# One encoder layer on one core: the delta rule's chunk step written as an affine map, and the head sums of keys and queries moved into the projection banks

## The chip, the cores and the metric

The kernel runs on one core of one Trainium2 chip. The metric is the device time of one execution in microseconds (us), the median of several runs. TensorE (PE) multiplies matrices into PSUM, which has eight banks of 128 x 512 numbers of 32 bits; VectorE (DVE) and ScalarE (ACT) work element by element and read PSUM; GpSimd (POOL) does the same between SBUF tiles, and the DMA queues move data between HBM and SBUF. PE's weight loads are listed apart, as PEld.

## The reference, cut to what matters

One layer of a streaming encoder for 1024 prompt frames and 64 sample frames. After a norm, one combined projection feeds four mixers in parallel (a conv module, a gated delta rule, a multi-scale pool, stick-breaking attention). Their outputs are concatenated, projected and added; a SwiGLU feed-forward follows. The change touches the scan of the delta rule and the norm of the attention's keys and queries.

```python
def chunk_gated_delta(q, k, v, g, beta, S0):
    ...
    sol = lax.linalg.triangular_solve(lmat + jnp.eye(CHUNK, dtype=jnp.float32), rhs,
                                      left_side=True, lower=True, unit_diagonal=True)
    u_c, w_c = sol[..., :Dv], sol[..., Dv:]
    ...
    def step(S, xs):
        u_i, w_i, attn_i, q_i, k_i, gl = xs
        v_new = u_i - jnp.einsum('bhcd,bhde->bhce', w_i, S)
        o = jnp.einsum('bhcd,bhde->bhce', q_i, S) + jnp.einsum('bhij,bhje->bhie', attn_i, v_new)
        S = S * gl[..., None, None] + jnp.einsum('bhcd,bhce->bhde', k_i, v_new)
        return S, o

def stick_breaking_mixer(u, k_prev, v_prev, qn_g, kn_g):
    B, L, _ = u.shape
    qkv = u.reshape(B, L, 3, SB_HEADS, SB_HEAD_DIM).transpose(2, 0, 3, 1, 4)
    q = rms_norm(qkv[0], qn_g)
    k = rms_norm(qkv[1], kn_g)
    ...
```

A chunk has 64 frames, there are four heads of width 64.

## The kernel before, in words

The frames are worked in two halves: half A is the first 512 prompt frames, half B the other 512 and the 64 of the sample. The program is written as: input projection of A, norm of B, mixers of A, input projection of B, mixers of B, output projection and feed-forward of A, then of B. A scheduler with a model of the machine decides the order in which the instructions of each engine stand, so projections of one half stand between the mixer steps of the other. Each engine executes its instructions in that order.

A projection (`gemm_fm`, tile `pg`) makes 128 output features in one PSUM tile for each piece of columns: one of 512 for half A, two of 288 for half B. Each operand is split into a high and a low part, so 8 blocks of input features give 24 matmuls. `gemm_bank` hands out the banks: at first the two of the pool `ps_mm`. The attention has three banks (`ps_sb`), the delta rule two (`ps_dn`, used through `PD` and `PS`), and `ps_cv` is a single bank, handed out by `PC`:

```python
    def PC(name):
        return ps_cv.tile([P, 512], F32, tag="cv", name=name)
...
            pm = PC("pmu")
...
            pm = PC("pvar")
...
                pp = PC("ppl")
```

These three tiles are the conv's mean and variance and the pool's small projection. A tile of a pool is handed out in the order of the program text, and the next use of the bank waits until the last has been read.

For keys and queries (`sb_qk`, four tiles to a half) ScalarE copies the projection to `qk` and its square to `qksq`; a matmul with a block of ones (`pqk`) sums the squares of a head, and ScalarE takes logarithm and exponent of it for the norm.

The delta rule (`delta`, `dn_group`) works groups of four chunks, two groups to a half, and one group of one chunk for the sample. A group makes the products of keys and queries (`pkk`, `pkq`), transposes keys and values by matmuls with an identity (`pkt`, `pvt`, and later `pw` from `X`, `pof`), and solves a triangular system: its diagonal blocks go by DMA to a layout that GpSimd solves row by row, and come back as `X`; the levels above are done by batches of matmuls (`pw`, `py`, `px`). `batch` issues 16 matmuls of 64 x 64 for four chunks, one for each chunk and head. Then `u` (`pu`) and the transposed `w` (`pwt`) are made, and the recurrence goes chunk by chunk: `pvn` = w S, `vn` = u - `pvn`, `pkv` = k `vn`, and the state S is scaled by ScalarE and added to by VectorE; the output `po` gathers q S and attention times `vn`.

Of the kernel before, what the change touches and what calls it, by code (L numbers as in the profile page):

```python
# [7 lines left out]
F32 = mybir.dt.float32  # L8
# [51 lines left out]
def hybrid_encoder_kernel(ctx: ExitStack, tc: tile.TileContext, io):  # L60
# [41 lines left out]
    def PC(name):  # L102
        return ps_cv.tile([P, 512], F32, tag="cv", name=name)
# [9 lines left out]
    def act_(out, in_, func, bias=0.0, scale=1.0):  # L113
        nc.scalar.activation(out, in_, func, bias=bias, scale=scale)  # L114

    def copy_a(out, in_):
        nc.scalar.activation(out, in_, ACTF.Copy)  # L117
# [4 lines left out]
    def tt(out, a, b, op):  # L122
        nc.vector.tensor_tensor(out=out, in0=a, in1=b, op=op)  # L123
# [13 lines left out]
    def mm(out, lhsT, rhs, start=True, stop=True):  # L137
        return nc.tensor.matmul(out, lhsT=lhsT, rhs=rhs, start=start, stop=stop)  # L138

    def mms(out, lhsT, rhs, start=True, stop=True):  # L140
        nc.tensor.matmul(out, lhsT=lhsT, rhs=rhs, start=start, stop=stop, skip_group_check=True)  # L141
# [193 lines left out]
    def gemm_bank(name="pg"):  # L335
        turn[0] += 1
        pool, tag = BANKS[turn[0] % 8] if wide[0] else BANKS[0]
        return pool.tile([P, 512], F32, tag=tag, name=name)
# [54 lines left out]
    def sb_qk(h):  # L393
        n_ = h.n
        for pi, piece in enumerate(("k", "q")):
            for m in range(2):
                ada_step(ADA_B if h.samp else ADA_N)
                t, sq = ST("qk"), ST("qksq")
                lo = ST("qkl") if piece == "k" else t
                tiles = gemm_fm(h, io["wfm"][14 + 2 * pi + m], h.hi, h.lo, KALL)  # L400
                with tc.high_priority():
                    for ps, c0, n in tiles:
                        copy_a(t[:, c0:c0 + n], ps[:, 0:n])
                        act_(sq[:, c0:c0 + n], ps[:, 0:n], ACTF.Square)
                    for c0, n in h.chunks:
                        pn = PC("pqk")
                        mm(pn[:, 0:n], C("bdones"), sq[:, c0:c0 + n])
                        act_(sq[:, c0:c0 + n], pn[:, 0:n], ACTF.Ln, bias=epst, scale=1.0 / 64)
                    act_(sq[:, 0:n_], sq[:, 0:n_], ACTF.Exp, scale=-0.5)
                    stt(t[:, 0:n_], t[:, 0:n_], gqk[:, pi:pi + 1], sq[:, 0:n_], ALU.mult, ALU.mult)  # L410
                    copy_a(sq[:, 0:n_].bitcast(F32R), t[:, 0:n_])
                    d = sbd[piece, h.name]
                    if piece == "k":
                        nc.sync.dma_start(out=io["sbk"][m, :, h.row0:h.row0 + n_], in_=t[:, 0:n_])
                    tt(lo[:, 0:n_].bitcast(F32R), t[:, 0:n_], sq[:, 0:n_], ALU.subtract)
                    for x, v in enumerate((sq, lo)):
                        if piece == "k":
                            for y in range(2):
                                nc.sync.dma_start(out=d[2 * m + y, 64 * x:64 * x + 64], in_=v[64 * y:64 * y + 64, 0:n_])
                        else:  # L420
                            nc.sync.dma_start(out=d[128 * m:128 * m + 128, x], in_=v[:, 0:n_])
# [265 lines left out]
    def dn_group(h, feats, gate, D, ch0, nch, tok0, mtok0, S):  # L687
# [7 lines left out]
        def v4(t):  # L695
            return t[:, 0:w].rearrange("p (a c d) -> p a c d", a=2, c=nch)
# [10 lines left out]
        def PS(name):  # L707
            return PD(name)
# [108 lines left out]
        batch(pwt, blk(kbe), blk(Y))  # L817
        wT = T4("X")
        copy_a(wT[:, 0:w], pwt[:, 0:w])
        po = ps_dn.tile([P, 512], F32, tag="dn", name="po")  # L820
        u4, o4 = v4(u), v4(po)
        for c in range(nch):
            pv2 = PS("pvn")
            for pair in range(2):
                j = (pair * nch + c) * 64
                for hp in range(2):
                    r = slice(64 * hp, 64 * hp + 64)
                    mm(pv2[r, pair * 64:pair * 64 + 64], wT[r, j:j + 64], S[r, pair])
                    mms(po[r, j:j + 64], qd[r, j:j + 64], S[r, pair], c == 0 and pair == 0, False)
            vn = dn.tile([P, 2, 64], F32, tag="vn", name="vn", bufs=2)  # L830
            tt(vn, u4[:, :, c], pv2[:, 0:128].rearrange("p (a d) -> p a d", a=2), ALU.subtract)
            for pair in range(2):
                act_(S[:, pair], S[:, pair], ACTF.Copy, scale=D["gl"][:, pair, ch0 + c:ch0 + c + 1])
            pk2 = PS("pkv")
            for pair in range(2):
                j = (pair * nch + c) * 64
                for hp in range(2):
                    r = slice(64 * hp, 64 * hp + 64)
                    mm(pk2[r, pair * 64:pair * 64 + 64], kup[r, j:j + 64], vn[r, pair])
                    mms(po[r, j:j + 64], at[r, j:j + 64], vn[r, pair], False, True)  # L840
            tt(S, S, pk2[:, 0:128].rearrange("p (a d) -> p a d", a=2), ALU.add)
        sq = T4("Y")
        act_(sq[:, 0:w], po[:, 0:w], ACTF.Square)
        ss = sm.tile([P, 2, 4], F32, tag="oss", name="oss")
# [510 lines left out]
```

## Time and profile before

| what | value |
|---|---|
| median of 3 runs | 1529.09 us (1527.38 to 1532.03) |
| the profiled execution | 1532.56 us, of it 1530.8 us from the first to the last instruction (span) |
| PE busy | 1459.6 us, 95% of the span |
| weight loads busy | 1259.9 us, 82% |
| VectorE busy | 1030.5 us, 67% |
| ScalarE busy | 663.2 us, 43% |
| GpSimd busy | 88.3 us, 6% |
| mean granted clock of TensorE | 0.953 of full speed |

Full speed is 2.4 GHz; the granted clock is a mean over a stretch, in which the engine runs at full or at half speed. A busy time is a sum over the whole span, in which stages with different limits follow one another; a busy PE also counts time at half clock, and the ends of pipelined matmuls. What a stage is worth is therefore read from windows, with the clock beside the busy time.

### The profile page before, as it was taken

How to read it: one execution, taken by the hardware profiler on the slowest of the kernel's cores; microseconds unless marked ns; L12 is line 12 of the kernel's file. 1: busy time of each engine (PE TensorE's matmuls, PEld its weight loads, DVE VectorE, ACT ScalarE, POOL GpSimd, SP SyncE). 2: the span in 40 equal slices, each digit the busy share in tenths (PEclk: the TensorE clock that was granted, in tenths of full speed). 3: DMA queues.
4: the chain of work that ended last, by engine and by line, in shares of the span. 5: the costliest groups of instructions: out<-in, count | busy, mean ns of one | idle time of the engine just before them, and what ended most of it. 6: DMA issues, size and time to landing. Idle time of an engine off the chain costs nothing.

```text
span 1530.8 us, 24538 instructions
## 1 busy us (share of the span) xinstructions
PE 1459.6 (95%) x9688; PEld 1259.9 (82%) x9688; DVE 1030.5 (67%) x1816; ACT 663.2 (43%) x1191; POOL 88.3 (6%) x196
## 2 busy tenths in 40 slices
PE   7899999958998989999999999999999999999999
PEld 5777799835896857677878778789899999999998
DVE  7877999865379997666766588744655555555554
ACT  4446554645454567466676442222432222222221
POOL 0000400030003000200300000000000000000000
PEclk7999999968897999699999999999999999999999
DMA  8796677432354213252323477622322222222222
GB/s 287 262 295 208 207 223 236 121 75 90 117 178 145 70 45 93 82 153 84 107 91 91 131 268 260 210 95 86 135 70 84 83 83 84 83 83 84 83 84 103
DMA packets 106867, 205.41 MB, mean 134 GB/s; under 512 B 39360, under 2 KB 49024, under 8 KB 106752
## 3 DMA queue, kind: packets, MB, share of 16 engines
q1 hardware_dynamic: 99936, 193.36, 39.1%
q0 software_dynamic: 6816, 10.49, 3.1%
q8 instruction: 76, 1.25, 0.3%
q14 instruction: 39, 0.32, 0.1%
HBM read 175.57 MB, written 28.24 MB: 133 GB/s over the span
## 4 chain that ended last, share of the span: by engine, by line
PE 70%; issue 11%; DMA 7%; DVE 6%; POOL 3%; ACT 2%; SPq 1%; DVEq 0%; POOLq 0%; ACTq 0%
PE pg L138 59%; PE psC L141 2%; POOL fst L135 1%; POOL fsu L135 1%; PE pw L138 1%; DVE junk L212 1%; PE psO L141 1%; PE z L141 1%; DVE wlo L123 1%; DMA out_sbk_dram<-qk 1%; DMA wadt<-in_wadat_dram 1%; DMA X<-xd 1%; DMA fsn<-nld 1%; DVE xA L126 1%; DVE nrm L126 1%
## 5 line engine op out<-in xcount | busy, mean ns | idle before, releaser
L138 PE MATMUL pg<-hi,whi 128*128 128x288 f32 (+1 forms) x1504 | 504.8, 336 | 7.6 <-ACT vf L117 3.3
L138 PE MATMUL pg<-hi,wlo 128*128 128x288 f32 (+1 forms) x1504 | 500.6, 334 | 4.8 <-DVE wlo L123 4.8
L138 PE MATMUL pg<-lo,whi 128*128 128x288 f32 (+1 forms) x1504 | 502.5, 334 | 1.7 <-DVE lo L126 1.6
L117 ACT ACTIVATE whi<-wraw 128x1024 fp32r<-128x1024 f32 (+2 forms) x192 | 199.7, 1041 | 488.2 <-PE pg L138 422.4
L138 PEld LDWEIGHTS pg<-hi,whi 128*128 128x128 f32 x1504 | 287.1, 191 | 35.5 <-ACT vf L117 4.1
L138 PEld LDWEIGHTS pg<-hi,wlo 128*128 128x128 f32 x1504 | 286.4, 191 | 29.9 <-DVE wlo L123 6.8
L138 PEld LDWEIGHTS pg<-lo,whi 128*128 128x128 f32 x1504 | 287.2, 191 | 27.9 <-issue 3.3
L123 DVE TENSOR_TENSOR wlo<-wraw,whi 128x1024 fp32r<-128x1024 f32 (+2 forms) x192 | 230.9, 1203 | 106.6 <-ACT whi L117 105.4
L138 PE MATMUL pg<-g,whi 128*128 128x288 f32 (+1 forms) x1056 | 253.1, 332 | 0.1
L138 PEld LDWEIGHTS pg<-g,whi 128*128 128x128 f32 x1056 | 180.0, 190 | 14.8 <-ACT acc L114 0.6
L138 PE MATMUL pg<-g,wlo 128*128 128x288 f32 (+1 forms) x528 | 173.1, 331 | 0.0
L126 DVE SCALAR_TENSOR_TENSOR xs<-pg,mod,xs 128x288 f32<-128x288 f32 (+2 forms) x288 | 106.5, 413 | 85.7 <-PE pg L138 82.5
L138 PEld LDWEIGHTS pg<-g,wlo 128*128 128x128 f32 x528 | 100.1, 190 | 7.8
L123 DVE TENSOR_TENSOR fa<-fa,pg 128x288 f32<-128x288 f32 (+1 forms) x66 | 35.0, 531 | 101.4 <-PE pg L138 98.2
L126 DVE SCALAR_TENSOR_TENSOR cy<-cvb,vec,cy 128x512 f32<-128x512 f32 (+1 forms) x120 | 94.2, 799 | 0.2
L126 DVE SCALAR_TENSOR_TENSOR xA<-pg,mod,xA 128x512 f32<-128x512 f32 x96 | 70.6, 747 | 22.8 <-PE pg L138 22.6
L212 DVE CUSTOM_DVE_ANT_0 junk<-wads,cb,vec 128x1024 bf16<-128x1024 f32 x32 | 41.0, 1282 | 17.6 <-DMA wads<-in_wadat_dram 12.8
L114 ACT ACTIVATE e<-e 128x512 f32<-128x512 f32 (+4 forms) x100 | 51.9, 519 | 0.8
L212 DVE CUSTOM_DVE_ANT_0 junk<-wadt,cb,vec 128x1024 bf16<-128x1024 f32 x32 | 41.0, 1282 | 16.3 <-DMA wadt<-in_wadat_dram 16.2
L138 PE MATMUL pg<-mixs,whi 128*128 128x288 f32 x256 | 50.9, 295 | 0.0
L114 ACT ACTIVATE zs<-zs 128x512 f32<-128x512 f32 (+4 forms) x50 | 25.7, 514 | 36.8 <-DVE zs L123 35.7
L138 PEld LDWEIGHTS pg<-mixs,whi 128*128 128x128 f32 x256 | 41.0, 188 | 0.1
(304 smaller groups left out, 1922.7 us busy)
## 6 DMA issues: line engine op xcount, KB each, us to landing
wraw<-in_wgate_dram SPq DMA_DIRECT2D x44, 512.0 KB, 3.7
wraw<-in_wup_dram SPq DMA_DIRECT2D x44, 512.0 KB, 3.8
wraw<-in_wdown_dram SPq DMA_DIRECT2D x44, 512.0 KB, 3.6
wadt<-in_wadat_dram SPq DMA_DIRECT2D x32, 512.0 KB, 5.0
wads<-in_wadat_dram SPq DMA_DIRECT2D x32, 512.0 KB, 4.5
wraw<-in_wfm_dram SPq DMA_DIRECT2D x30, 512.0 KB, 4.3
wraw<-in_wout_dram SPq DMA_DIRECT2D x16, 512.0 KB, 3.7
xA<-in_xa_dram SPq DMA_DIRECT2D x16, 256.0 KB, 6.7
```

The lines of the kernel that those rows point to most:

```text
L114: nc.scalar.activation(out, in_, func, bias=bias, scale=scale)
L117: nc.scalar.activation(out, in_, ACTF.Copy)
L123: nc.vector.tensor_tensor(out=out, in0=a, in1=b, op=op)
L126: nc.vector.scalar_tensor_tensor(out, a, s, b, op0, op1)
L135: nc.gpsimd.tensor_tensor(out=out, in0=a, in1=b, op=op)
L138: return nc.tensor.matmul(out, lhsT=lhsT, rhs=rhs, start=start, stop=stop)
L141: nc.tensor.matmul(out, lhsT=lhsT, rhs=rhs, start=start, stop=stop, skip_group_check=True)
L212: nc.vector.tensor_tensor_reduce(out=junk, in0=w, in1=cbt[g], scale=1.0, scalar=V("b_ada", col), op0=ALU.mult, op1=ALU.add, accum_out=mod[ ...
```

## The change

It has two parts. In `sb_qk` the head sum's tile comes from `gemm_bank` instead of `PC`. In `dn_group` the step over a chunk becomes an affine map of the state: S' = k u + M S with M = gl I - k w, and M is made for all four chunks at once (`pww` is w itself, `pmt` is k w, `gi` the scaled identity, `mt_` the difference). The loop over chunks holds the two matmuls of the map, summed in PSUM (`pst`), and one copy to the next state; all states stay in `Sc`. What hung on the states (`pvn`, `vn`, `po`) then follows in batches.

```diff
@@ sb_qk
-                        pn = PC("pqk")
+                        pn = gemm_bank("pqk")
                         mm(pn[:, 0:n], C("bdones"), sq[:, c0:c0 + n])
@@ dn_group
-        po = ps_dn.tile([P, 512], F32, tag="dn", name="po")
-        u4, o4 = v4(u), v4(po)
+        pw2 = PS("pww")
+        batch(pw2, blk(Y), blk(kbe))
+        wt_ = T4("W")
+        copy_a(wt_[:, 0:w], pw2[:, 0:w])
+        gi = T4("vb")
+        tt(v4(gi), bc(D["gl"]), C("sel2")[:, 0:64].unsqueeze(1).unsqueeze(1).to_broadcast(sh4), ALU.mult)
+        pm = PS("pmt")
+        batch(pm, blk(wt_), blk(kup))
+        mt_ = T4("Y")
+        tt(mt_[:, 0:w], gi[:, 0:w], pm[:, 0:w], ALU.subtract)
+        Sc = T4("kbe")[:, 0:128 * nch].rearrange("p (c a d) -> p c a d", c=nch, a=2)
+        copy_a(Sc[:, 0], S)
+
+        def each(c):
+            for pair in range(2):
+                for hp in range(2):
+                    yield pair, slice(64 * hp, 64 * hp + 64), (pair * nch + c) * 64
+
         for c in range(nch):
-            pv2 = PS("pvn")
-            for pair in range(2):
-                j = (pair * nch + c) * 64
-                for hp in range(2):
-                    r = slice(64 * hp, 64 * hp + 64)
-                    mm(pv2[r, pair * 64:pair * 64 + 64], wT[r, j:j + 64], S[r, pair])
-                    mms(po[r, j:j + 64], qd[r, j:j + 64], S[r, pair], c == 0 and pair == 0, False)
-            vn = dn.tile([P, 2, 64], F32, tag="vn", name="vn", bufs=2)
-            tt(vn, u4[:, :, c], pv2[:, 0:128].rearrange("p (a d) -> p a d", a=2), ALU.subtract)
-            for pair in range(2):
-                act_(S[:, pair], S[:, pair], ACTF.Copy, scale=D["gl"][:, pair, ch0 + c:ch0 + c + 1])
-            pk2 = PS("pkv")
-            for pair in range(2):
-                j = (pair * nch + c) * 64
-                for hp in range(2):
-                    r = slice(64 * hp, 64 * hp + 64)
-                    mm(pk2[r, pair * 64:pair * 64 + 64], kup[r, j:j + 64], vn[r, pair])
-                    mms(po[r, j:j + 64], at[r, j:j + 64], vn[r, pair], False, True)
-            tt(S, S, pk2[:, 0:128].rearrange("p (a d) -> p a d", a=2), ALU.add)
+            pS = PS("pst")
+            for pair, r, j in each(c):
+                mms(pS[r, pair * 64:pair * 64 + 64], kup[r, j:j + 64], u[r, j:j + 64], pair == 0, False)
+            for pair, r, j in each(c):
+                mms(pS[r, pair * 64:pair * 64 + 64], mt_[r, j:j + 64], Sc[r, c, pair], False, True)
+            nxt = S if c == nch - 1 else Sc[:, c + 1]
+            copy_a(nxt, pS[:, 0:128].rearrange("p (a d) -> p a d", a=2))
+        pv2 = PS("pvn")
+        for c in range(nch):
+            for pair, r, j in each(c):
+                mm(pv2[r, j:j + 64], wT[r, j:j + 64], Sc[r, c, pair])
+        vn = T4("W")
+        tt(vn[:, 0:w], u[:, 0:w], pv2[:, 0:w], ALU.subtract)
+        po = PS("po")
+        o4 = v4(po)
+        for c in range(nch):
+            for pair, r, j in each(c):
+                mms(po[r, j:j + 64], qd[r, j:j + 64], Sc[r, c, pair], c == 0 and pair == 0, False)
+        for c in range(nch):
+            for pair, r, j in each(c):
+                mms(po[r, j:j + 64], at[r, j:j + 64], vn[r, j:j + 64], False, True)
```

Since the scheduler sets the order, it moves far more than these lines. First, PE's order in half A's second delta group, from the attention's steps to the first use of the solved `X` (the `pw` with a number; `z`, `psC` and `psO` are the attention, `pvar` the conv). Before:

```order
L138 MATMUL pvar<-cvs,cst 128x256 x2
L141 MATMUL psC<-sl,u_r 128x384
L141 MATMUL z<-q_2693,k_2691 128x128 x2
L141 MATMUL z<-neg_r,id_r 128x128
L141 MATMUL psC<-sh,omu_r 128x384
L141 MATMUL psC<-sl,omu_r 128x384
L141 MATMUL psO<-zs,v_2594 64x384
L141 MATMUL psC<-sh,u_r 128x512
L141 MATMUL psC<-sl,u_r 128x512
L728 MATMUL pw_2130<-cst,X 64x64
```

The same place of the change:

```order
L138 MATMUL pvar<-cvs,cst 128x256
L138 MATMUL pg<-hi_1356,whi 128x288
L138 MATMUL pg<-lo_1357,whi 128x288
L138 MATMUL pg<-hi_1356,wlo 128x288
L138 MATMUL pg<-hi_1364,whi 128x288
L138 MATMUL pg<-lo_1365,whi 128x288
L138 MATMUL pg<-hi_1364,wlo 128x288
L138 MATMUL pg<-hi_1372,whi 128x288
L138 MATMUL pg<-lo_1373,whi 128x288
L138 MATMUL pg<-hi_1372,wlo 128x288
L138 MATMUL pg<-hi_1380,whi 128x288
L141 MATMUL z<-q_2775,k_2773 128x128
```

Between the last `pkk` of this group and that `pw` stand 2 projection matmuls (`pg`) before and 167 of the change. In the second group of half B there are 45 before and 114 of the change, in its first group 48 of 512 columns and 72 of 288 before and 126 of 512 of the change.

Second, PE's order in half A at its first key tile, whose last matmul is `pg<-hi_564,wlo`. The row with + is the head sum, which stood behind the next tile's 24 matmuls:

```order
 L138 MATMUL pg<-lo_565,whi 128x512
 L138 MATMUL pg<-hi_564,wlo 128x512
+L138 MATMUL pqk<-qksq,cst 128x512
 L138 MATMUL pg<-hi_277,whi 128x512
 L138 MATMUL pg<-lo_278,whi 128x512
```

Third, PE's order in the recurrence of half A's first group. Before, one chunk's first half (`X` is the tile that holds w by then):

```order
L138 MATMUL pg<-hi_1340,wlo 128x288
L138 MATMUL pvn<-S_p,X 64x64
L141 MATMUL po<-S_p,qd 64x64
L138 MATMUL pvn<-S_p,X 64x64
L141 MATMUL po<-S_p,qd 64x64
L138 MATMUL pvn<-S_p,X 64x64
L141 MATMUL po<-S_p,qd 64x64
L138 MATMUL pvn<-S_p,X 64x64
L141 MATMUL po<-S_p,qd 64x64
L141 MATMUL psC<-sh,u_r 128x384
```

Of the change, the end of one chunk's map and the beginning of the next (`nl` is the tile that holds u, `kbe` the one of the states):

```order
L138 MATMUL pg<-lo_1373,whi 128x288
L141 MATMUL pst<-kbe,Y 64x64 x4
L141 MATMUL pst<-nl,kup 64x64 x4
L141 MATMUL psC<-sh,omu_r 128x384
L141 MATMUL psC<-sl,omu_r 128x384
L138 MATMUL pg<-hi_1372,wlo 128x288
```

A chunk had two such blocks of eight; it now has one, with 30 or so projection and attention matmuls to the next. Blocks of 64 x 64 matmuls between wider ones number 83 in PE's whole order before and 95 of the change. GpSimd's order changes in one place: the solve of half A's second group stood behind the loads of all four heads of the attention, and now stands ahead of the fourth head's.

## Rows read from the trace of the kernel before

**Rows 1.** Windows: length, busy us (instructions) by engine, clock, DMA share, GB/s.

```profile
100.00:304.40 204.40, 201.73 (x1543) 169.23 (x1541) 177.12 (x324) 115.41 (x235) 21.70 (x39) 0.98 0.66 208
304.40:400.00 95.60, 68.22 (x585) 47.57 (x583) 53.13 (x120) 44.24 (x97) 15.44 (x37) 0.76 0.31 86
...
458.90:660.00 201.10, 188.73 (x1220) 141.99 (x1220) 170.30 (x290) 114.53 (x219) 26.01 (x66) 0.86 0.30 88
...
1120.00:1530.80 410.80, 406.91 (x3068) 406.67 (x3068) 205.08 (x393) 93.53 (x127) 0.00 (x0) 1.00 0.26 86
```

**Rows 2.** Timeline of PE: start, duration, operation, count, idle before and releaser.

```profile
304.40 0.29 PE L138 MATMUL pg<-hi,wlo 128*128 128x288 f32 x1
...
341.39 0.31 PE L728 MATMUL pw<-cst,X 64*64 64x64 f32 x1 [10.32 <-DMA X<-xd]
343.79 0.47 PE L138 MATMUL pw<-cst,X 64*64 64x64 f32 x2 [2.08 <-DMA X<-xd]
...
372.34 0.65 PE L138 MATMUL pqk<-qksq,cst 128*128 128x288 f32 x2
...
382.86 0.85 PE L138 MATMUL pg<-hi,whi 128*128 128x288 f32 x1
```

**Rows 3.** Timeline of ScalarE, half B's first key tile to A's last pool result.

```profile
281.69 0.41 ACT L117 ACTIVATE qk<-pg 128x288 f32<-128x288 f32 x1 [1.57 <-PE pg L138]
...
287.33 0.40 ACT L114 ACTIVATE qksq<-pg 128x288 f32<-128x288 f32 x1
...
371.22 0.69 ACT L114 ACTIVATE plm<-ppl,vec 128x512 f32<-128x512 f32 x1 [0.84 <-PE ppl L138]
```

**Rows 4.** PE's waits, for whom: us in total, times, longest us.

```profile
PE pw L728 <- DMA X<-xd: 13.8, 2, 10.3
PE pqk L138 <- ACT qksq L114: 5.8, 4, 2.7
...
PE pvn L138 <- DVE S_p L123: 1.7, 2, 1.1
```

**Rows 5.** Timeline of PE, two batches of 16 small matmuls and what follows.

```profile
364.18 1.15 PE L138 MATMUL pu<-vb,Y 64*64 64x64 f32 x32
365.16 1.10 PE L138 MATMUL pwt<-Y,kbe 64*64 64x64 f32 x32
366.19 0.44 PE L141 MATMUL psC<-sl,u_r 128*128 128x384 f32 x1
```

**Rows 6.** Timeline of PE, into and out of a block of eight small matmuls.

```profile
233.62 0.29 PE L138 MATMUL pg<-hi,whi 128*128 128x288 f32 x1
233.84 0.34 PE L138 MATMUL pkv<-vn,kup 64*64 64x64 f32 x4
...
234.50 0.40 PE L138 MATMUL pg<-lo,whi 128*128 128x288 f32 x1
234.74 0.29 PE L138 MATMUL pg<-hi,wlo 128*128 128x288 f32 x1
```

**Rows 7.** Timeline of ScalarE behind half A's first key tile.

```profile
108.41 1.06 ACT L117 ACTIVATE whi<-wraw 128x1024 fp32r<-128x1024 f32 x1 [1.13 <-PE pg L138]
...
109.86 0.59 ACT L114 ACTIVATE qksq<-pg 128x512 f32<-128x512 f32 x1
```

**Rows 8.** Windows around the arrival of X, in the columns of rows 1.

```profile
301.49:341.39 39.90, 23.72 (x154) 15.52 (x153) 28.86 (x60) 21.52 (x44) 13.22 (x33) 0.68 0.32 77
475.00:495.00 20.00, 15.60 (x90) 11.93 (x89) 17.19 (x31) 10.65 (x20) 0.00 (x0) 0.74 0.36 95
610.00:645.00 35.00, 32.67 (x151) 23.08 (x151) 24.58 (x52) 16.10 (x33) 8.87 (x30) 0.66 0.31 85
```

**Rows 9.** Groups of VectorE by form: count, busy us, mean ns.

```profile
L123 DVE TENSOR_TENSOR W<-pw,cst 128x512 f32<-128x512 f32 x8 | 5.5, 688 | 4.9 <-PE pw L138 4.9
...
L123 DVE TENSOR_TENSOR vn<-nl,pvn 128x128 f32<-128x128 f32 x17 | 4.9, 286 | 3.3 <-PE po L141 3.2
```

**Rows 10.** Chain that ended last, one projection tile: start us, us, what.

```profile
124.21 5.58 PE pg L138 x24
```

## The prediction

> **What bounds the kernel now.** I read the trace by stage first, because the share of busy time hides stages with different limits. In [rows 1] each line gives a stretch's length, the busy time of every engine and the clock that TensorE (PE) was granted. Length minus PE's busy time multiplied by the clock is, roughly, time that PE lost by standing still or by running at half its clock. The last stretch, 410.8 us, loses under 4: the feed-forward layers are nothing but matmuls. Stretch 100 to 304.4 loses 204.4 - 201.73 x 0.98 = 7 us, and there VectorE is busy 177 of 204. But 304.4 to 400 loses 95.6 - 68.22 x 0.76 = 44 us, and 458.9 to 660 loses 201.1 - 188.73 x 0.86 = 39 us. So PE bounds the kernel, and the two weak stretches are the only large reserves, 83 us together.
>
> The timeline of PE says what the first hole is [rows 2]. A projection matmul (`pg`) starts at 304.40, and the next one at 382.86. In the 78 us between, PE has only the attention of half A, its second delta group, conv and pool, each of which waits for itself. At 341.39 PE has stood 10.3 us waiting for the solved block `X`. Why did the projections of half B stop? ScalarE's rows answer [rows 3]: the first key tile of half B was copied and squared at 281.69 to 287.73, but the head sum `pqk` that needs the squares starts only at 372.34 [rows 2], right after ScalarE read the last pool result `ppl` at 371.22 to 371.91 [rows 3]. Conv, pool and head sums share the pool `ps_cv` of one PSUM bank, and banks are given out in program order: half B's head sum must wait until half A's conv and pool are through. The projections of the later tiles stand behind that sum in PE's order, and so they wait too: 85 us for a bank, not for data.
>
> The list of PE's waits shows the opposite for the recurrence [rows 4]: the wait for the state in `pvn` comes to 1.7 us in 2 cases, while `X` costs 13.8 and `pqk` 5.8. The recurrence has matmuls of other work around it, so shortening its chain returns next to nothing.
>
> **The change, part by part.** *Added matmuls.* A group of four chunks issued 64 matmuls of 64 x 64 in the recurrence (16 `pvn`, 16 `pkv`, 32 `po`). It now issues 16 `pww`, 16 `pmt`, 32 `pst`, 16 `pvn`, 32 `po`: 112. That is 48 more in each of four groups and 12 in the one-chunk sample group: 204. A batch of 16 (32 records, two to a matmul) takes from 364.18 to 365.16 and the next one to 366.19, so 1.03 us [rows 5]. 204 / 16 x 1.03 = +13 us. In stages where PE is the bound this is paid in full. The lower bound, if all of it fell into holes, is 0.
>
> *Switches between shapes.* From the projection matmul at 233.62 to the second one behind a block of eight small ones, at 234.74, is 1.12 us [rows 6]. Two projections at 0.13 (406.9 us / 3068 in the last line of [rows 1]) and eight small ones at 0.0625 explain 0.76, so entering and leaving the block costs 0.36 more. The order of PE's instructions has 83 such blocks before and 95 after: 12 x 0.36 = +4 us. The Trainium skill ("TensorEngine Tiling (Array Packing)", Tiling Modes) says that changing the tiling mode drains the engine; by it all of those 0.36 us are due at each block, whoever feeds it. Read as a wait on `vn`, which the row alone doesn't exclude, they would cost nothing and the sum would be 4 lower.
>
> *VectorE and ScalarE.* Removed for each group of four: eight small VectorE steps (`vn` and the state, 0.286 each, 2.3 us [rows 9]) and eight short ScalarE scalings. Added: three wide VectorE steps at 0.69 (2.1 us, the row of `W<-pw` in [rows 9]), two wide ScalarE copies near 0.59 (the wide step in [rows 7]) and five narrow ones near 0.4 ([rows 3]). Both engines come out even, and I take 0. The covers are the projections that stand between the `pst` blocks in the new order; without them a chunk would expose one copy and its hand-over, under 1 us.
>
> *Head sums in the projection banks, half A.* In the order before, a head sum stands one tile (24 matmuls) behind its own. Now it stands directly behind it. ScalarE frees PE's last tile at 108.41, then converts a weight, copies `qk` and squares it until 110.45 [rows 7]: 2.0 us in which PE waits, four times. Behind it three of the four have other small work ahead of the head sum (`pgc` and one `pl`; `pl` and `pgcb`; `pkk` and `pkq`, 1.3 to 2.1 us), so some 3 us stay, and about 1 to 2 us of the 5.8 us that `pqk` waits today [rows 4] go. Net +2, between 0 and +8.
>
> *Head sums, half B.* Here the hole closes. The new order has 167 projection matmuls between the second group's `pkk` and its first use of `X`, where two stood. At 0.1326 us they are 22 us. Today this stretch, 301.49 to 341.39, holds 23.72 x 0.68 = 16 us of work in 40 [rows 8]. 16 + 22 = 38 us, against the 42 that `X` needs from `pkk` at 301.49 to 343.79 [rows 2, 8]: PE will wait little for `X`. Of the 44 us lost I take 33 as regained. Kept are 4 us of waiting, some 5 at half clock (the transposes stay in pairs of batches, and PE is granted low clocks around them today, 0.68 on average in [rows 8]) and 2 for the new head sums. The bounds are 16, when VectorE can't follow (see below), and 40.
>
> *Half B's delta groups.* Their stages lose 20 - 15.60 x 0.74 = 8.5 us at 475 to 495 and 35 - 32.67 x 0.66 = 13.4 at 610 to 645 [rows 8], both around the arrival of `X`. In the new order the stretch from `pkk` to the first use of `X` holds 126 matmuls of 512 columns in the first group (before: 48, and 72 narrow ones) and 114 (before: 45) in the second. 24 of them take 5.58 us [rows 10], so 16 us more work stands before the second group's `X` and some 9 before the first's. I take 13 of the 22 as regained: half the hole is half clock, which more work shortens but doesn't remove. Bounds: 0, since these matmuls are missing elsewhere, and 22.
>
> **The sum.** 13 + 4 + 2 - 33 - 13 = -27 us, so the span goes from 1530.8 to 1504. The profiled execution took 1532.56 in all and the median of the runs is 1529.09, 3.5 lower, so the median after is 1532.56 - 27 - 3.5 = 1502.
>
> **The rivals.** *VectorE becomes the bound* (chance 0.20). It is busy 87% in 100 to 304.4 [rows 1]; the conv steps that now idle along in the hole must then fit beside denser work. Against it: in 304.4 to 400 it is busy only 53 of 96 us. If half of the 33 is lost to it, the time is 1518.
>
> *The reserve is larger* (0.15). All `X` waits and the half clock behind them go: 5 us more in half A and 15 more of the 39 in 458.9 to 660 [rows 1]: 1482.
>
> *Slower: the head sums now hold the projections back* (0.10). `pqk` takes one of only two banks of `ps_mm` and keeps it until ScalarE's logarithm. In half B each of four tiles has two of them, eight places at which PE, in order, can stand before a head sum or before the next projection. The whole gain of 27 is gone when each costs 27 / 8 = 3.4 us. Today's longest wait of a head sum is 2.7 us [rows 4]; if the 2.0 for evacuating a tile [rows 7] come on top at every place, 8 x 4.7 = 38, the time is 1540. Against it: the new order puts attention or delta matmuls ahead of most of these sums.
>
> *The hole only moves* (0.04): the projections spent early are missing later, the losses return behind them, and the added 19 are matched: 1530, no change.
>
> My forecast has the remaining 0.51, with its own range 1490 to 1513. The range for 8 in 10 reaches from 1480, below the larger reserve, to 1524, above the case of VectorE; the two last rivals stay outside. A difference of 0.3%, some 4.6 us, is about what can be told from no change. Faster by more than that: 0.51 + 0.20 + 0.15 = 0.86; the same 0.03 and slower 0.11, from the last two rivals.
>
> **What would show it.** In the changed profile the gap between projection matmuls of half B is at most a few us anywhere before the output projection; PE's busy share there is above 0.95 and `pw` waits under 6 us for `X`. The output projection of half A (at 458.9 today, the border in [rows 1]) begins some 25 to 45 us earlier. Batches of `pww`, `pmt` and `pst` cost about 1 us for 16. `pqk` in half A waits near 2 us at the first tile. I am wrong if the list of PE's waits names `pqk` with over 15 us, if VectorE's share in the delta groups of half A passes 0.95 while PE idles, or if the stretch of half B's two groups loses 39 us as before.

## The result, and the profile of the changed kernel

The changed kernel takes 1541.69 us in the median (1530.71 to 1548.50, 14 runs), the kernel before 1529.57 us in the same session. The ratio is 1.0079, with a 95% interval from 1.0054 to 1.0104. A second series, run beside the first experiments, gave 1536.16 us against 1528.03, a ratio of 1.0063 (1.0034 to 1.0092). (A ratio in this document is not exactly the quotient of the two medians beside it; the two differ by up to 0.2%.) The change makes the kernel 0.6 to 0.8% slower, where 1502 us were forecast.

The first profiled execution took 1533.88 us, 7.8 below its median, so against the 1532.56 us of before it shows only a small part of the difference. What it shows is where time went. First the windows with the borders of [rows 1], and one more from 660 to 1120 us.

```profile
100.00:304.40 204.40, 192.75 (x1529) 158.91 (x1527) 164.59 (x291) 106.89 (x217) 18.41 (x39) 0.95 0.63 199
304.40:400.00 95.60, 91.36 (x828) 73.29 (x827) 59.98 (x116) 56.01 (x123) 15.84 (x39) 0.95 0.46 131
458.90:660.00 201.10, 183.45 (x1253) 139.18 (x1254) 166.43 (x274) 115.57 (x216) 34.52 (x70) 0.93 0.28 83
660.00:1120.00 460.00, 444.40 (x2575) 366.84 (x2574) 300.33 (x465) 209.19 (x357) 20.41 (x44) 0.97 0.42 134
```

For the last of these the kernel before has this row:

```profile
660.00:1120.00 460.00, 450.99 (x2448) 372.64 (x2446) 310.69 (x482) 220.30 (x377) 23.67 (x48) 0.99 0.45 140
```

Length minus PE's busy time multiplied by the clock is the lost time, as in the prediction. (The clock has two digits, so a stretch of 460 us is good to some 2 us.) The hole lost 44 us and loses 95.6 - 91.36 x 0.95 = 9. The stretch of half B's two groups lost 39 and loses 201.1 - 183.45 x 0.93 = 30. But 100 to 304.4 lost 7 and loses 204.4 - 192.75 x 0.95 = 21, and 660 to 1120 lost 460 - 450.99 x 0.99 = 14 and loses 460 - 444.40 x 0.97 = 29. So 44 us came back where they were expected, and 29 went in two stretches that I had counted at 2 and 0. From 0 to 100 us, outside these windows, the loss is 100 - 84.10 x 0.88 = 26 us before and 100 - 86.89 x 0.95 = 17 here, but 22 in a second profiled execution of the changed kernel (e4), so part of that varies from one execution to the next. This execution is 1.3 us longer than that of before. That leaves 16 to 25 us for the added matmuls and for what this arithmetic can't tell.

The list of PE's waits of the changed kernel answers to [rows 4]: for whom, us in total, times, longest.

```profile
PE pw L728 <- DMA X<-xd: 12.6, 2, 9.0
PE pg L138 <- DVE wlo L123: 6.6, 6, 2.1
PE pv L138 <- DVE lo L126: 5.3, 3, 3.5
...
PE pqk L138 <- ACT qksq L114: 5.0, 6, 2.5
PE pg L138 <- ACT whi L117: 3.6, 5, 0.9
```

The waits of the head sum are no longer than before, 5.0 against 5.8 us, and the one of the first tile is 2.5. The recurrence doesn't appear among the long waits, nor does the hole: the first wait for `X` of half A's second group has gone. What is new is `lo` (the low parts of half B's norm, for the projection `pv`), and a wait of 9.0 for `X` in half B's first group.

The new loss at 100 to 304.4 us can be followed on three engines. Half B's norm has two sums (`pn`), one in a bank of the delta rule and one in the single bank (`pn = (PD if pns else PC)("pn")`; so the single bank has one more user than the three tiles named with the kernel before). In the kernel before the one in the single bank comes after the four head sums:

```profile
147.02 0.75 PE L138 MATMUL pn<-acc,cst 128*128 128x288 f32 x2
```

In the changed kernel both stand at 73.58, since the single bank is free of head sums:

```profile
73.58 1.13 PE L138 MATMUL pn<-acc,cst 128*128 128x288 f32 x4
...
182.75 0.59 PE L138 MATMUL pv<-whi,hi 128*128 128x264 f32 x1 [0.97 <-ACT hi L114]
183.53 0.59 PE L138 MATMUL pv<-whi,lo 128*128 128x264 f32 x1 [0.20 <-DVE lo L126]
188.06 0.59 PE L138 MATMUL pv<-whi,lo 128*128 128x264 f32 x1 [3.50 <-DVE lo L126]
191.58 0.59 PE L138 MATMUL pv<-whi,lo 128*128 128x264 f32 x1 [1.64 <-DVE lo L126]
```

The norm has its sums 73 us earlier and yet PE waits for its last steps at 183 to 192. ScalarE's timeline says why:

```profile
171.15 0.58 ACT L117 ACTIVATE ust<-pg 128x512 f32<-128x512 f32 x1
181.45 0.63 ACT L114 ACTIVATE cve<-cvg 128x512 f32<-128x512 f32 x1 [9.72 <-DMA cvg<-ucvA]
181.99 1.80 ACT L114 ACTIVATE hi<-xB,mod 128x512 fp32r<-128x512 f32 x4
```

ScalarE stands 9.72 us before the conv's second input, which goes to HBM and back, and the norm's high parts `hi` stand behind it in its order. In the kernel before, eight of these `hi` steps stand ahead of that `cve`, and it doesn't wait:

```profile
168.08 0.95 ACT L114 ACTIVATE hi<-xB,mod 128x512 fp32r<-128x512 f32 x2
...
169.60 2.65 ACT L114 ACTIVATE hi<-xB,mod 128x512 fp32r<-128x512 f32 x6
172.16 0.61 ACT L114 ACTIVATE cve<-cvg 128x512 f32<-128x512 f32 x1
```

In the stretch 660 to 1120, one kind of wait can be shown, and it explains little. The rows before PE's waits for `wlo` (the low part of a weight), VectorE first:

```profile
884.33 1.28 DVE L212 CUSTOM_DVE_ANT_0 junk<-wads,cb,vec 128x1024 bf16<-128x1024 f32 x1 [2.13 <-DMA wads<-in_wadat_dram]
...
887.64 1.22 DVE L123 TENSOR_TENSOR wlo<-wraw,whi 128x1024 fp32r<-128x1024 f32 x1
```

```profile
886.12 0.50 PE L138 MATMUL pg<-hi,whi 128*128 128x512 f32 x1 [0.92 <-ACT whi L117]
888.92 0.79 PE L138 MATMUL pg<-hi,wlo 128*128 128x512 f32 x1 [2.06 <-DVE wlo L123]
```

`junk` is the modulation of the sample, which reads its own weights by DMA, and `wlo` stands behind it. PE's waits for `wlo` come to 6.6 us in the whole kernel and to 4.8 in the kernel before, so they are some 2 of the 15 us that this stretch loses more. The rest isn't traced to a wait: PE's busy time in it fell by 6.6 us, and the granted clock is 0.97 where it was 0.99.

### The profile page after: what moved, and what is told of

It is laid out like the page before. It is cut to its first block, busy times and chain, and to the rows that moved or that the text cites. A ratio compares the mean times of both kernels' runs of the same rounds, so it can differ in the third digit from the quotient of the medians.

```text
span 1532.0 us, 25329 instructions
## 1 busy us (share of the span) xinstructions
PE 1464.1 (96%) x10096; PEld 1263.7 (82%) x10096; DVE 1028.7 (67%) x1797; ACT 660.2 (43%) x1184; POOL 89.4 (6%) x196
## 4 chain that ended last, share of the span: by engine, by line
PE 74%; DVE 11%; DMA 7%; issue 3%; POOL 2%; ACT 2%; SPq 1%; DVEq 0%; POOLq 0%; ACTq 0%
PE pg L138 57%; PE pk L138 2%; PE psC L141 2%; DMA wads<-in_wadat_dram 1%; DVE cy L126 1%; PE psO L141 1%; DVE wlo L123 1%; DVE junk L212 1%; PE pw L138 1%; PE z L141 1%; DVE xA L126 1%; PE pv L138 1%; PE pmod L138 1%; DMA wadt<-in_wadat_dram 1%; POOL fst L135 1%
## 5 line engine op out<-in xcount | busy, mean ns | idle before, releaser
L114 ACT ACTIVATE fa<-pg 128x288 f32<-128x288 f32 (+1 forms) x52 | 22.3, 429 | 40.1 <-PE pg L138 40.1
```

## The experiments

Each kernel is compared with the kernel before, run beside it on the same chip.

**The two parts alone (e1, e2), the price of the added matmuls (e3), and the changed kernel again (e4).** e1 is the first edit of the change alone, e2 the affine map alone:

```diff
-                        pn = PC("pqk")
+                        pn = gemm_bank("pqk")
```

> Head sums in the two projection banks, recurrence of before. Theory 1 (the hole's time is really won, the affine map spends it again): no added matmuls, the hole closed as in the changed kernel; time 10 to 20 us below before, ratio 0.987 to 0.993. Theory 2 (the hole only moves: the work that would fill it is missing later): within 5 us of before, ratio 0.997 to 1.003, with the losses back behind 400 us. Theory 3 (head sums hold the projections back in the two banks): slower than before by 5 us or more.

Measured: 1536.41 us against 1528.03, ratio 1.0047 (1.0023 to 1.0072). The head sums alone, which add no work, are slower. Theory 1 falls. Theory 2 misses the time narrowly (its band ends at 1.003, inside the interval), though losses did come back behind 400 us: the stretch from 660 to 1120 loses 460 - 429.08 x 0.96 = 48 us. Theory 3 has the sign; what it names doesn't show, since PE's waits for `pqk` are 3.9 us in 4 cases. The hole is closed. One wait is new, where the feed-forward of half A borrows a bank from the attention:

```profile
871.37 0.28 PE L141 MATMUL psOs<-pl,v2s 128*128 128x64 f32 x1
889.75 0.77 PE L138 MATMUL pg<-hi,whi 128*128 128x512 f32 x1 [18.10 <-DVE sbo L123]
```

The sample's attention gives its bank back only after four results have gone out one after the other (`sbo`); a projection that is handed this bank waits 18.1 us.

> Affine recurrence, head sums in the single bank of before. Theory 1: slower than before by 22 to 32 us (1.014 to 1.021), so that it and the head sums add up to the 12 us measured. Theory 2 (only the 204 added matmuls count): slower by 10 to 17 us (1.007 to 1.011). The hole of some 80 us without projections must be there again in both.

Measured: 1527.25 us against 1528.03, ratio 0.9974 (0.9948 to 1.0000). So the affine map doesn't cost what it adds, and both theories fall on this point too. The windows show where its work is paid:

```profile
304.40:400.00 95.60, 80.44 (x707) 58.25 (x707) 49.40 (x109) 46.00 (x103) 13.78 (x37) 0.79 0.33 85
458.90:660.00 201.10, 192.75 (x1442) 146.51 (x1441) 176.08 (x290) 118.67 (x222) 24.90 (x60) 0.92 0.31 93
```

The hole is there but loses 95.6 - 80.44 x 0.79 = 32 us, not 44, and half B's groups 201.1 - 192.75 x 0.92 = 24, not 39 [rows 1]. So time returns in both places; whether the shorter recurrence, the added matmuls or the new order returns it is not separated.

In e3, on the kernel of e1, the batch for the transposed w is issued four times into the same tile; nothing reads the repeats:

```diff
-        batch(pwt, blk(kbe), blk(Y))
+        for _ in range(4):
+            batch(pwt, blk(kbe), blk(Y))
```

> Recurrence of before and head sums in the projection banks; the batch that makes the transposed w is issued four times into the same tile instead of once, so 48 matmuls of 64 x 64 more in each group of four chunks and 12 in the sample's: the 204 that the affine map adds, with nothing that waits on them. If the matmuls alone are the cost of the affine map, it stands 13 us above the kernel with the head sums alone and at the time of the changed kernel (some 1.008 of before). If the affine map's waits, copies or places in the order cost more, it is well below the changed kernel; if the gaps take the matmuls up, within 4 us of the head sums alone.

Measured: 1539.85 us, ratio 1.0080 (1.0048 to 1.0112). That is the time of the changed kernel, as expected for matmuls alone, but only 0.3% above e1 and not 13 us, and e1 holds a wait of 18 us that the others don't. e10 asks again.

> The changed kernel once more, on the same chip as the three others, so that they can be compared with it: ratio 1.005 to 1.011 by every theory. Its profile should show which losses vary from execution to execution: the first profiled execution was 8 us below the median, at a clock of 0.969.

Measured: 1.0063, as told above. The profiled execution of this series took just the median, 1536.16 us, and has the same new waits.

**Head sums by halves (e5, e6), with the affine map (e7), and with later borrowing (e8).** The traces suggested a fourth theory: the two halves of the head sums do opposite things. e5 and e7 leave half A's in the single bank (e7 with the affine map), e6 half B's. `h.samp` is true for half B. The edit is that of e7 on the changed kernel; e5 writes the same line into the kernel before, and e6 writes it there with `gemm_bank` and `PC` exchanged:

```diff
-                        pn = gemm_bank("pqk")
+                        pn = (gemm_bank if h.samp else PC)("pqk")
```

> Recurrence of before; only half B's head sums go to the two projection banks, half A's stay in the single bank. Theory 4 (read from the traces of the first four): half B's sums close the hole and return 25 to 30 us between 300 and 400, half A's cost some 12 us between 100 and 200 (PE waits for the sum of the first tile, and ScalarE stands 7 to 10 us before the conv's second input with the norm of half B queued behind it). Then this kernel loses nothing between 100 and 200 and stands 10 to 25 us below before, 0.984 to 0.993. Rival (closing the hole only moves its loss behind 480 us, wherever half A's sums are): within 5 us of before, 0.997 to 1.003.

> The complement: only half A's head sums in the projection banks, half B's in the single bank, recurrence of before. By theory 4 the hole is there as before, the stretch from 100 to 200 loses 10 to 15 us more than before, and the time is 8 to 15 us above before, 1.005 to 1.010. If half A's sums are harmless, the time is within 4 us of before.

> Half B's head sums in the projection banks and the affine recurrence. The affine map alone paid for its added work (0.997). If that holds beside the closed hole too, this is the fastest: 15 to 30 us below before, 0.980 to 0.990. If the affine map got its work back only out of the hole that is now closed, it stands 10 to 17 us above the kernel with half B's head sums alone.

Measured: half B's alone 1506.40 us against 1527.48, ratio 0.9878 (0.9846 to 0.9910). Half A's alone 1537.31, ratio 1.0082 (1.0052 to 1.0112). Half B's and the affine map 1518.20, ratio 0.9945 (0.9922 to 0.9969). Both halves come out in theory 4's bands of time; whether its waits are the cause is the question of e9 and e12. e7 is the second of its two cases: the affine map costs 0.9945 / 0.9878 = 1.0068, some 10 us, give or take 6, once the hole is closed. The windows of e5, and the one from 400 us of the kernel before:

```profile
100.00:304.40 204.40, 202.03 (x1488) 168.91 (x1486) 174.14 (x320) 112.51 (x231) 20.16 (x39) 0.96 0.66 205
304.40:400.00 95.60, 93.58 (x809) 78.13 (x809) 66.67 (x124) 56.61 (x121) 14.75 (x39) 0.93 0.51 139
400.00:458.90 58.90, 55.51 (x308) 43.90 (x308) 56.80 (x105) 33.84 (x76) 0.00 (x0) 0.88 0.49 156
458.90:660.00 201.10, 190.90 (x1195) 143.93 (x1191) 160.29 (x278) 122.85 (x234) 28.78 (x72) 0.89 0.34 93
660.00:1120.00 460.00, 448.98 (x2583) 373.63 (x2584) 290.51 (x452) 202.90 (x340) 19.31 (x42) 0.97 0.42 132
```

```profile
400.00:458.90 58.90, 58.90 (x449) 54.87 (x448) 35.49 (x58) 33.66 (x68) 1.30 (x3) 0.96 0.51 160
```

The hole loses 95.6 - 93.58 x 0.93 = 9 and half B's groups 31, as in the changed kernel; 100 to 304.4 loses 204.4 - 202.03 x 0.96 = 10 where the changed kernel loses 21. Yet of 35 + 8 regained only some 19 us (1.22%) stay. The 8 come from the border at 458.9 us: from 400 to there e5 loses 58.9 - 55.51 x 0.88 = 10 us and the kernel before 58.9 - 58.90 x 0.96 = 2, so from 400 to 660 us both lose 41, and half B's groups regain nothing in e5. From 660 to 1120 it loses 25, 11 more than before.

In e8 half A's feed-forward borrows banks two pairs of tiles later, on the kernel of e1:

```diff
-WIDE = 6
+WIDE = 8
```

> Head sums of both halves in the projection banks, recurrence of before, and the feed-forward of half A borrows the banks of attention and delta rule only from its ninth pair of tiles on (WIDE 8, was 6). With the head sums alone PE stood 18.1 us at 889.75 for a borrowed bank that the sample's attention still held. If that wait is what made the head sums alone slower, this kernel is 15 to 20 us below that one, 1518 us, 0.993 of before; if it only took the place of other waits (half A's sums, late weights), it is within 5 us of it, 1.002 to 1.007.

Measured: 1519.11 us, ratio 0.9944 (0.9919 to 0.9969), by the ratios some 16 us below e1. The wait for the borrowed bank is gone, and the time with it. But the changed kernel has no such wait, and so this explains e1 and not the result. One thing more bears on which bank is borrowed: `gemm_bank` counts its calls, and from the borrowing on the count modulo eight picks the bank. Half A's four sums, once they call it, move every later pick by four; half B's eight move none. Whether that brought the wait of e1 is not tested.

**One wait taken away (e9), the matmuls again (e10), a control (e11).** In the changed kernel, e9 places the conv's second sigmoid behind the last `hi` step on ScalarE:

```diff
-            sigmoid_chain(e[:, 0:h.n], g[:, 0:h.n])
+            with tc.issue_after(HB.hi_last) if i == 1 and not h.samp else nullcontext():
+                sigmoid_chain(e[:, 0:h.n], g[:, 0:h.n])
```

> The changed kernel with one order more: on ScalarE the sigmoid of half A's second conv input is placed behind the last step that makes the high parts of half B's norm (hi). If the 8 to 10 us that ScalarE stands before the conv's input with the norm queued behind it are what half A's head sums cost, the stretch from 100 to 200 loses some 18 us instead of 28, and the kernel is 8 to 12 us below the changed one, 1.000 of before, give or take 0.003. If those waits are covered anyhow, or the loss goes elsewhere, it stays within 4 us of the changed kernel, 1.005 to 1.009.

Measured: 1539.81 us against 1529.31, ratio 1.0053 (1.0017 to 1.0089): 0.1 to 0.3% below the changed kernel, give or take 0.5, so no gain that stands clear of the noise. The edit did its work where it was made. The windows of e9, and then the one from 400 us of the changed kernel:

```profile
100.00:304.40 204.40, 197.03 (x1567) 162.77 (x1565) 170.91 (x306) 107.85 (x218) 17.05 (x39) 0.97 0.63 202
...
400.00:458.90 58.90, 53.58 (x415) 45.16 (x413) 51.30 (x97) 34.38 (x76) 0.00 (x0) 0.94 0.51 169
```

```profile
400.00:458.90 58.90, 57.52 (x460) 48.92 (x456) 46.49 (x91) 34.84 (x73) 0.00 (x0) 0.97 0.55 176
```

The first stretch loses 204.4 - 197.03 x 0.97 = 13 us and no longer 21. From 400 to 458.9 it loses 58.9 - 53.58 x 0.94 = 9 where the changed kernel loses 58.9 - 57.52 x 0.97 = 3, so most of the 8 us went right behind the hole, and the rest within what two digits of clock can tell. Taking the visible wait of the first stretch away did not bring the 8 to 12 us; e12 and e13 come back to it.

e10 is e5 with the edit of e3, e11 is e5 with the edit of e8.

> Half B's head sums in the projection banks, recurrence of before, and the batch that makes the transposed w issued four times into the same tile: the 204 added matmuls of the affine map with nothing that waits on them, on the kernel that has neither the hole nor the wait for a borrowed bank. If the matmuls are the whole cost of the affine map there, it stands 10 to 15 us above half B's head sums alone (0.9878 of before) and level with half B's head sums plus the affine map: 0.994 to 0.997. If the map's copies and waits are part of it, 0.988 to 0.991.

Measured: 1532.92 us, ratio 1.0011 (0.9983 to 1.0038), 1.3% or 20 us above e5: more than the affine map with as many matmuls (e7). One wait is new, 6.4 us of `psC` for VectorE at 238.01, 11 us behind such a block of 64; that the block causes it is not shown. Between e3, e7 and e10 the price of 204 matmuls is 5 to 20 us; 13 is not contradicted and not confirmed.

> Half B's head sums in the projection banks, recurrence of before, and the later borrowing of banks (WIDE 8). A control: its trace without it shows no wait for a borrowed bank, so if such a wait was what the later borrowing removed with the head sums of both halves (1.0047 to 0.9944), nothing changes here, 0.986 to 0.990. If the later borrowing helps for another reason, it gains here too, 0.976 to 0.982.

Measured: 1519.15 us, ratio 0.9932 (0.9903 to 0.9960): 0.5% slower than e5. The later borrowing doesn't help by itself, as the first case had it, but it isn't neutral either: an edit that removes no wait moved the time by 8 us. It is no change of order alone, since the feed-forward has fewer banks for two pairs of tiles, and its list of PE's waits has 5.2 us for `xA`, 2.9 for `g` and 2.8 for `fa`, where e5 has 1.3, none and none.

e11 also gives e8 its counterpart: they differ only in half A's sums. Their first windows, e8 first:

```profile
100.00:304.40 204.40, 197.75 (x1414) 163.90 (x1413) 162.95 (x294) 103.55 (x212) 18.31 (x39) 0.93 0.64 203
```

```profile
100.00:304.40 204.40, 201.72 (x1498) 168.37 (x1497) 175.25 (x321) 113.32 (x235) 22.34 (x39) 0.97 0.66 205
```

e8 loses 204.4 - 197.75 x 0.93 = 20 us there and e11 204.4 - 201.72 x 0.97 = 9, and the norm's sums stand at 74.79 in e8, as early as in the changed kernel. Yet the ratios are 0.9944 and 0.9932: here half A's move costs 0.1%, give or take 0.4, where with the borrowing of before (e1 against e5) it costs 1.7%.

**What in half A's move costs (e12, e14), and what the order edit of e9 costs by itself (e13).** e12 is the changed kernel with half A's sums in a bank of the attention that nobody uses then; e13 is e7 with the edit of e9, where there is no wait to remove; e14 is e7 with the norm's first sum in that attention bank:

```diff
 # e12
-                        pn = gemm_bank("pqk")
+                        pn = gemm_bank("pqk") if h.samp else ps_sb.tile([P, 512], F32, tag="o", name="pqk")
 # e14
-            pn = (PD if pns else PC)("pn") if early else gemm_bank("pn")
+            pn = (PD("pn") if pns else ps_sb.tile([P, 512], F32, tag="o", name="pn")) if early else gemm_bank("pn")
```

> The changed kernel, but half A's head sums take a bank of the attention that is idle then, neither the two of the projections nor the single one. If holding the projection banks is what half A's sums cost, this stands with the kernel that leaves them in the single bank: 0.990 to 0.998 of before. If the cost comes with leaving the single bank, through the order of what follows, it stands with the changed kernel: 1.004 to 1.010.

Measured: 1547.62 us against 1528.60, ratio 1.0115 (1.0080 to 1.0150). That is just above its second band and not faster than the changed kernel, so holding the projection banks is not what half A's sums cost. ScalarE's wait before the conv's second input is only 1.21 us here, at 167.86, with eight `hi` steps ahead of it: the kernel is slow without the wait that e9 took away.

> Half B's head sums and the affine map (0.9945) with the order of ScalarE that was forced in the ninth run: half A's second sigmoid behind the norm of half B. Here no wait stands there to be removed, so by its mechanism nothing changes, 0.992 to 0.997. The order of the program behind it changes all the same; if such a change alone is worth 5 to 15 us, the time moves out of that band, and a difference of this size between two kernels can't be given to one wait.

Measured: 1528.06 us, ratio 0.9988 (0.9963 to 1.0013), 0.4% above e7. This is the second case: the edit costs some 6 us, give or take 5, where it removes no wait. It isn't quite idle, since the conv's `cve` now starts behind all `hi` steps, at 176.53 and not at 169.12 as in e7. The same price may hide a gain of that size in e9, so e9 by itself doesn't settle what the wait was worth.

> Half B's head sums and the affine map; half A's sums stay in the single bank, but the norm of half B takes its first bank from the attention and so can move some 70 us ahead, as in the changed kernel. If the early norm is what half A's move cost, it is as slow as the changed kernel, 1.003 to 1.010; if not, it stays at 0.990 to 0.998.

Measured: 1533.41 us, ratio 1.0026 (1.0001 to 1.0052), 0.8% or 12 us above e7, between its two cases. Here the head sums of half A take the single bank as before, and the edit moves only the norm of half B: `pn` stands at 70.33, in e7 at 144.15. The windows say that the cost isn't in one place:

```profile
100.00:304.40 204.40, 195.38 (x1534) 159.85 (x1533) 169.13 (x302) 106.59 (x218) 19.69 (x39) 0.95 0.63 200
304.40:400.00 95.60, 91.57 (x777) 73.75 (x775) 55.38 (x105) 54.92 (x120) 12.51 (x37) 0.90 0.46 122
458.90:660.00 201.10, 190.22 (x1231) 143.56 (x1233) 161.44 (x270) 114.93 (x216) 35.65 (x70) 0.89 0.27 80
660.00:1120.00 460.00, 439.65 (x2570) 360.83 (x2567) 300.32 (x463) 208.45 (x358) 21.44 (x44) 0.98 0.42 136
```

For e7 the same windows read:

```profile
100.00:304.40 204.40, 200.61 (x1611) 166.94 (x1610) 175.81 (x316) 108.73 (x222) 25.98 (x46) 0.97 0.64 201
304.40:400.00 95.60, 92.52 (x890) 76.88 (x891) 56.22 (x106) 59.17 (x129) 13.06 (x33) 0.95 0.47 136
458.90:660.00 201.10, 188.48 (x1494) 143.97 (x1495) 167.09 (x272) 121.92 (x233) 24.99 (x56) 0.95 0.32 91
660.00:1120.00 460.00, 447.71 (x2443) 372.19 (x2444) 295.96 (x454) 204.24 (x341) 18.17 (x42) 0.99 0.42 135
```

By the same arithmetic e14 loses 19, 13, 32 and 29 us, e7 10, 8, 22 and 17. These sums overstate the difference: e14's profiled execution is the slowest of its 12 (1542.07 us), that of e7 (1512.92) the second fastest of its 12, so they lie 29 us apart and the medians 15.

## Why the prediction was wrong, by its own steps

**Two steps failed. By size the larger is what half B's head sums return: "Of the 44 us lost I take 33 as regained" and "13 of the 22", 46 us together; alone they return some 19 (e5). The other is "Head sums in the projection banks, half A": "Net +2, between 0 and +8".** With the affine map's 10 instead of 17, the measured terms give -19 + 10 + 18 to 21 = +9 to +12 us. (They add up to the result because each is the step from one kernel to the next: e5 from before, e7 from e5, the changed kernel from e7.)

**Half A, +2.** Half A's move costs 1.0082 on its own (e6, some 13 us), and in the changed kernel 1.0063 or 1.0079 over the 0.9945 of e7, that is 1.2 to 1.3%, 18 to 21 us. Without it the kernel is faster than before. The wait that I priced came as I priced it, 2.5 us at the first tile and 5.0 in all. What I didn't price is that the single bank also serves the norm of half B: once the head sums leave it, the norm's sum moves 73 us ahead in the order, and everything behind is ordered anew. Moving the norm alone costs 12 us (e14); moving the sums to a bank where they hold nothing up costs as much as in the changed kernel (e12). So in this kernel the cost comes with leaving the single bank and not with holding the two others, and of the 1.2 to 1.3% the early norm alone brings 0.8. But it is no fixed price: with the later borrowing and the recurrence of before, the same move with the same early norm costs 0.1%, give or take 0.4 (e8 against e11). That suggests that the order of the work far behind decides what is paid; which waits add up to it is not shown, and the cause stays open. The one that I could name, ScalarE before the conv's input, is not enough: it was taken away without a clear gain (e9), and e12 is as slow with 1.2 us of it. The pick of borrowed banks, which half A's four calls of `gemm_bank` move, isn't enough either, since e12 and e14 don't move it and are slow.

**Half B's hole, -33:** the mechanism and the size in place were right. The hole went from 44 us to between 7 and 13 in both profiles of the changed kernel and in e1, e5 and e7, and with half A's sums left alone the kernel is 1.2% faster (e5). The gap between projection matmuls of half B before the output projection is at most 8.4 us (331.15 to 339.57), where it was 78. **Half B's groups, -13** (0 to 22): 39 became 30 in the changed kernel, so -9. But e5, with the head sums alone, loses as much as before from 400 to 660 us, so the head sums, to which I gave the 13, don't bring it by themselves; e2, with the affine map alone, has 24 us in place of 39. The wait for `X` isn't under 6 us, since it is 9.0 in the first group. The output projection of half A begins at 438.3 us, 20.6 earlier and not 25 to 45. So the sum failed beyond half A: of the 35 us regained in the hole only 19 stayed, and 660 to 1120 us loses 11 more than before. I had the rival for this, "the hole only moves", and gave it 4 in 100. About half of it is true.

**Added matmuls +13, and switches +4:** the affine map costs 10 us where the hole is closed (e7 over e5), give or take 6, so it doesn't tell the 13 from the 17. The timeline of the changed kernel has a batch of 16 from 381.20 to 382.18, so 0.98 us, as said. By the Trainium skill ("TensorEngine Tiling (Array Packing)", Tiling Modes) each of the twelve added blocks would drain the engine; no run separates that part. But on the kernel before, the map costs nothing (e2, 0.9974): its work fits into the hole and into half B's groups. That contradicts "shortening its chain returns next to nothing". It returns about what it adds, as long as the head sums haven't closed the hole. So the two parts draw on the same reserve; since my sum gave the reserve to the head sums and charged the map in full, this is not where it failed.

**VectorE and ScalarE, 0:** right, though the change adds one wide ScalarE copy to a group and not two. Their busy times are 1028.7 and 660.2 us, before 1030.5 and 663.2. VectorE's share from 100 to 304.4 is 164.59 / 204.4 = 81%, less than the 87% before, and so it is not the bound.

**The rival on the slower side** gave 1540 us, close to the result, and was wrong in its mechanism, so the number was luck: head sums that hold the projections back. Their waits are as short as before, and e12 frees the banks without any gain.

**What limits all of this.** An edit that removes no wait moved the time by 0.4% (e13 over e7) and 0.5% (e11 over e5); neither is a change of order alone. Half B's gain (1.2%) is two to three times as large. Half A's loss runs from 0.1% (e8 over e11) over 0.8% (e6) and 1.2 to 1.3% (the changed kernel over e7) to 1.7% (e1 over e5). Differences of a few us between two of these programs say nothing on a single wait.

The best kernel of the study is e5, half B's head sums alone: 0.9878 of before.

## What to carry to other kernels

Before you move a tile out of a shared bank, list every other user of that bank, in the program's order: what you free is handed to the next of them, and that may be work you did not mean to move. Try such a move separately for each stage, since the same line closed a hole in one half, worth 19 us, and cost some 13 us in the other. And where a scheduler orders the program anew, a sum of stalls read from the trace is good for the place of a gain, but what stays of it must be measured, against a control edit that changes as little as possible besides the order.

## What I had not expected of the hardware

The time of one program largely goes with the granted clock of the execution: of the changed kernel, 1530.71 us came with a mean clock of 0.965 and 1548.50 with 0.954 (but 1540.03 with 0.966). The profiled execution had 0.969, the highest of its 14, and so was a flattering one; its difference from before, 1.3 us, was a tenth of that of the medians.
